# A hybrid attention and S5 block: the scan's output matmuls and the merge transposes held in groups, the rotation phases' low part and two placings on ScalarE, the attention scale in the rotation tables

## The chip, the cores and the metric

One core of a Trainium2 chip. The metric is device time in microseconds (us) of one execution, as the median over repeated runs.

## The reference

One block of a decoder over 256 tokens of width 1024, in float32: an attention branch and a state-space branch run on the same normed input, are merged by gates, and an MLP follows.

```python
h = rms_norm(x, g_mix);  q, k, v, u, g = split(h @ w_in)      # w_in: 1024 x 5632
q, k = rotary(q), rotary(k)                                    # 8 heads of 128
s = q @ k.T * HEAD_DIM ** -0.5                                 # causal, one block of 256
o_a = softmax(s) @ v
# S5: 32 groups of 16 channels, 64 complex states each
x_t = a * x_{t-1} + c * (B u_t);   y = C x + d_skip * u        # a = exp(lam * step), complex
o_b = glu(gelu(y) @ w_glu)
x = x + (sigmoid(g_a) * o_a + sigmoid(g_b) * o_b) @ w_out
x = x + square(relu(rms_norm(x, g_mlp) @ w_up)) @ w_down
out = rms_norm(x, g_final)
```

## The kernel before

**Projections.** Every weight is read once, in units of 128x1024 (512 KB) that `w_load` brings in on SP's queue into five `raw` buffers. `split` (L82 to L85) cuts a unit into two parts: `hi`, a cast on ScalarE (L83), and `lo` = raw - hi, a subtraction on VectorE (L84). Each product is then three matmuls in fp32r (hi·hi, hi·lo, lo·hi): `mm3` (L88 to L90, 256 columns) for q, k, the gate g and up, `tok_mm` (L267 to L269, 512 columns) for v, gb, glu and wo. There are four `hi` and four `lo` buffers. TensorE thus needs, for each unit, a cast of ScalarE and a subtraction of VectorE in time.

**The scan.** The complex recurrence over the 32x64 states is turned into two real scans in a frame that rotates with the state. `prepare` computes the state's constants on VectorE in 128x16 tiles (`s...`), builds the input matrices `Bs` (GpSimd memsets, copies `bpad`, and `place` puts the products `ab` beside it), transposes them on TensorE (`bt`, L471) and copies them to `W2` (L472). A second part builds the output matrices `Wr`, `nWi` and `Dt` with further placings. `tables(m)` makes cos and sin of the phases of a quarter m of the states: angle `ang` in tile `tha` from a high part (`uhi`, four ScalarE activations, L516) and a low part (four VectorE operations, L520), then `cs` and `sn` on ScalarE. `ssm_quad(m)` runs a quarter: matmuls `x` (L539), rotation on VectorE, eight scans (L555, L556), rotation back to `sr` and `si`, and the output matmuls into `y`: `Dt` on the inputs `U2` (L568), `Wr` on `sr` and `nWi` on `si` (L574, 64 columns of the array each).

**Attention.** `rope` turns q and k with the tables `rcos` and `rsin` (L297 to L299), `attn_head` forms scores `s` (L307 to L312), their maximum (L314 to L316), exponentials and the scaled `pr`; `attn_pt` transposes `pr` (`pt`, L330), `attn_out` multiplies with v (`o`).

**Merge.** For each of four groups of channels, glu is projected, gated, multiplied with the gate `thb`, and transposed in four transposes `mt` (L662).

**Order.** The parts are written in the order of `ORDER`, but each engine's final order is set when the kernel is built: a scheduler simulates the engines and issues by priority (weight splits at `SPLIT_PRIO`, attention at `ATT_PRIO`). On the chip every engine then runs its list strictly in that order. A different operation or dependency can therefore move instructions far from the edited lines.

Of the kernel before, what the change touches and what calls it, by code (L numbers as in the profile page):

```python
# [16 lines left out]
P = 128  # L17
# [31 lines left out]
def build(ctx, tc, dr, out):  # L49
# [182 lines left out]
    rs_par = rs.rearrange("p (j e) -> p e j", e=2).unsqueeze(1).to_broadcast([P, 2, 2, P])  # L232
    for c in range(2):
        V.tensor_mul(u[:, 2 * c : 2 * c + 2], by_parity(u_acc[:, c]), rs_par)
    V.tensor_mul(rcos, cos_c, rs)
    V.tensor_mul(rsin, sin_c, rs)
    for q in range(4):
        for e in range(2):
            r = 64 * (q % 2) + 32 * e
# [59 lines left out]
        V.tensor_add(o, o, sw)  # L299
        return o  # L300

    scale = P ** -0.5
    mixA = p1.tile([P, KD, T], F32, name="mixA")

    def attn_head(q, k, j):
        s = att_bank("s").rearrange("p a b -> p (a b)")
        PE.matmul(s[:, 0:128], q[:, j, 0:128], k[:, j, 0:128], start=True, stop=False,  # L307
                  skip_group_check=True)
        PE.matmul(s[:, 0:128], ident_b, tri_b, start=False, stop=True, skip_group_check=True)
        PE.matmul(s[:, 128:384], q[:, j, 128:256], k[:, j, :], start=True, stop=False,  # L310
                  skip_group_check=True)
        PE.matmul(s[:, 256:384], ident_b, tri_b, start=False, stop=True, skip_group_check=True)  # L312
        st = p1.tile([P, 6], F32, tag="st", bufs=2, name="st")
        V.tensor_reduce(st[:, 0:1], s[:, 0:128], axis=mybir.AxisListType.X, op=ALU.max)  # L314
        V.tensor_reduce(st[:, 1:2], s[:, 128:384], axis=mybir.AxisListType.X, op=ALU.max)
        V.tensor_scalar(st[:, 0:2], st[:, 0:2], -scale, None, op0=ALU.mult)  # L316
        pr = p1.tile([P, 384], F32, tag="pr", bufs=2, name="pr")
        act(pr[:, 0:128], s[:, 0:128], AF.Exp, bias=st[:, 0:1], scale=scale,
                     accum_out=st[:, 2:3])
        act(pr[:, 128:384], s[:, 128:384], AF.Exp, bias=st[:, 1:2], scale=scale,  # L320
                     accum_out=st[:, 3:4])
        V.reciprocal(st[:, 4:6], st[:, 2:4])
        S.activation(pr[:, 0:128], pr[:, 0:128], AF.Copy, scale=st[:, 4:5])
        S.activation(pr[:, 128:384], pr[:, 128:384], AF.Copy, scale=st[:, 5:6])
        return pr

    def attn_pt(pr):
        pt = att_bank("pt").rearrange("p a b -> p (a b)")
        for i in range(3):
            PE.transpose(pt[:, i * P : (i + 1) * P], pr[:, i * P : (i + 1) * P], ident)  # L330
        pts = p1.tile([P, 384], F32, tag="pts", bufs=2, name="pts")
        S.copy(pts, pt[:, 0:384])
        return pts

    def attn_out(hp, prs, tha):
        pts = [attn_pt(x) for x in prs]
        o = att_bank("o")
        for j in range(2):
            hd = 2 * hp + j
            PE.matmul(o[:, j, :], v[:, 0, hd * P : (hd + 1) * P], pts[j][:, 0:256],  # L340
                      start=True, stop=False, skip_group_check=True)
# [17 lines left out]
    def prepare():  # L359
# [89 lines left out]
            V.tensor_mul(w, x_r, wide(y_i))  # L449
            (V.tensor_sub if neg_i else V.tensor_add)(o_i, o_i, w)  # L450

        def place(dst, k, src):
            for g in range(2):
                r = slice(64 * g, 64 * (g + 1))
                G.tensor_scalar(dst[r, :, k + 16 * g : k + 16 * (g + 1)], src[r], 1.0, None,
                                    op0=ALU.mult)

        Bs = [p1.tile([P, ST, 64], F32, tag=f"y{c}", name=f"Bs{c}") for c in range(2)]
        ab = [compact(f"ab{c}") for c in range(2)]
# [49 lines left out]
    def rot(name, bufs=1):  # L509
        return p1.tile([P, 4, P], F32, tag=name, bufs=bufs, name=name)  # L510

    def tables(m):
        hi, nlo = ssm[-2:]
        uhi, ang, cs, sn = rot("q", QK), rot("tha", 2), rot("cs", 4), rot("sn", 4)
        for q in range(4):
            S.activation(uhi[:, q, :], tpos, AF.Copy, scale=hi[:, 4 * m + q : 4 * m + q + 1])  # L516
        V.tensor_scalar(ang, uhi, -0.1, MAGIC, op0=ALU.add, op1=ALU.add)
        V.scalar_tensor_tensor(ang, ang, MAGIC, uhi, op0=ALU.subtract, op1=ALU.subtract)
        for q in range(4):
            V.scalar_tensor_tensor(ang[:, q, :], tpos, nlo[:, 4 * m + q : 4 * m + q + 1],  # L520
                                   ang[:, q, :], op0=ALU.mult, op1=ALU.add)
# [8 lines left out]
    def ssm_quad(m):  # L530
# [29 lines left out]
        V.tensor_sub(sr, sr, w)  # L560
        V.tensor_mul(si, b, sn)
        V.tensor_mul(w, d, cs)
        V.tensor_add(si, si, w)
        Wr, nWi, Dt = ssm[1:4]
        y = bank("y", 1, "y")
        for h in range(2):
            p = 2 * m + h
            PE.matmul(y[:, h, 0:P], Dt[:, p, :], U2[:, p, 1 : P + 1], start=(h == 0), stop=False,  # L568
                      skip_group_check=True)
        for i, (w_, s_) in enumerate(((Wr, sr), (nWi, si))):  # L570
            for h in range(2):
                for j in range(2):
                    q = 2 * h + j
                    PE.matmul(y[64 * j : 64 * (j + 1), h, 0:P], w_[:, 4 * m + q, :], s_[:, q, :],  # L574
                              start=False, stop=(i == 1), skip_group_check=True)
        if m < 3:
            S.copy(ysb[:, m], y[:, :, 0:P])
        for q in range(4):
# [66 lines left out]
    for q in range(4):  # L645
        acc = wide_banks(f"glu{q}") if q % 2 else [flat(mm_bank(f"glu{q}{h}")) for h in range(2)]
        for kk_ in range(2):
            wh, wl = w_unit(dr["w_glu"][2 * q + kk_], f"glu{q}{kk_}")
            for k2 in range(2):
                k, w = 2 * kk_ + k2, slice(k2 * 512, (k2 + 1) * 512)  # L650
                for hf in range(2):
                    tok_mm(acc[hf], wh[:, w], wl[:, w], yhl[0][:, 0:4], yhl[0][:, 4:8], k, hf,
                           k == 0, k == 3)
        tp = att_bank(f"mt{q}")
        for hf in range(2):
            sg = p1.tile([P, T], F32, tag=f"ab{hf}", name="sg")
            act(sg, acc[hf][:, 256:512], AF.Tanh, scale=0.5)
            V.scalar_tensor_tensor(sg, sg, 1.0, acc[hf][:, 0:256], op0=ALU.add, op1=ALU.mult)
            tb = thb[q][:, hf, :]
            V.scalar_tensor_tensor(tb, tb, 1.0, sg, op0=ALU.add, op1=ALU.mult)  # L660
            for i in range(2):
                PE.transpose(tp[:, i, hf * P : (hf + 1) * P], tb[:, i * P : (i + 1) * P], ident)  # L662
        two = slice(2 * q, 2 * q + 2)
        V.scalar_tensor_tensor(mixA[:, two, :], tp, 0.5, mixA[:, two, :],
                               op0=ALU.mult, op1=ALU.add)
# [218 lines left out]
```

## Time and profile before

| what | value |
|---|---|
| median of three runs | 397.4 us (397.14 to 397.8) |
| the profiled execution | 396.13 us |
| its span, first to last instruction | 394.3 us |
| mean granted clock of TensorE, share of full | 0.996 |
| TensorE busy | 384.7 us, 98% |
| VectorE busy | 293.0 us, 74% |
| ScalarE busy | 225.9 us, 57% |
| GpSimd busy | 30.9 us, 8% |

The span lies 1.8 us under the profiled execution's time, and that execution 1.3 us under the median. A busy share is an average over the whole span; the kernel's stages differ.

### The profile page before, as it was taken

The page shows a single profiled execution, that of the slowest core. Times are in us where ns is not written, and L with a number is a line of the kernel's source. Part 1 is how long each engine was busy: PE and PEld are TensorE (multiplying, and loading weights), DVE is VectorE, ACT ScalarE, POOL GpSimd, SP SyncE. Part 2 cuts the span into 40 slices and gives each one's busy share as a digit, 9 for nine tenths or more (in the row PEclk, how much of TensorE's full clock was granted, in tenths as well). Part 3 has the DMA queues.
Part 4 walks back from the last instruction along what each step waited for, and adds up shares of the span by engine and source line. Part 5 has one row for each costly group of instructions (what it writes and reads, how often), then busy time and mean ns, then how long its engine had stood idle before and what let it go on. Part 6 is the DMA issues. An engine that isn't in the chain of part 4 may idle for free.

```text
span 394.3 us, 6719 instructions
## 1 busy us (share of the span) xinstructions
PE 384.7 (98%) x2563; PEld 344.5 (87%) x2563; DVE 293.0 (74%) x521; ACT 225.9 (57%) x360; POOL 30.9 (8%) x39
## 2 busy tenths in 40 slices
PE   8999999999999999999999999999999999999993
PEld 5988898999899787888889999999999888888883
DVE  5989999999999996659748677666676444563434
ACT  6857976664366665945636755655655434344313
POOL 4261491000000000000000000000000000000000
PEclk9999999999999999999999999999999999999998
DMA  8994743354625255347396386656556555565202
GB/s 275 374 342 147 248 161 107 108 173 160 215 72 183 91 166 161 118 152 236 140 324 214 106 267 208 193 185 211 187 190 211 173 204 192 184 211 177 89 2 106
DMA packets 23199, 71.57 MB, mean 181 GB/s; under 512 B 2944, under 2 KB 5248, under 8 KB 23168
## 3 DMA queue, kind: packets, MB, share of 16 engines
q1 hardware_dynamic: 20144, 68.92, 52.5%
q10 hardware_dynamic: 3024, 2.23, 2.0%
q8 instruction: 20, 0.33, 0.3%
q14 instruction: 11, 0.09, 0.1%
HBM read 69.18 MB, written 1.05 MB: 178 GB/s over the span
## 4 chain that ended last, share of the span: by engine, by line
PE 79%; DVE 10%; DMA 3%; issue 3%; ACT 2%; POOL 1%; ACTq 1%; SPq 0%
PE up L90 7%; PE up L89 7%; PE up L88 7%; PE dn L734 6%; PE dn L735 6%; PE dn L736 6%; PE gb L269 2%; PE gb L267 2%; PE gb L268 2%; PE glu L269 2%; PE glu L267 2%; PE wo L268 2%; PE glu L268 2%; PE wo L267 2%; PE wo L269 2%
## 5 line engine op out<-in xcount | busy, mean ns | idle before, releaser
L89 PE MATMUL up<-x2l,hi_up 128*128 128x256 f32 x256 | 70.7, 277 | 0.0
L90 PE MATMUL up<-x2h,lo_up 128*128 128x256 f32 x256 | 70.6, 277 | 0.0
L88 PE MATMUL up<-x2h,hi_up 128*128 128x256 f32 x256 | 70.1, 277 | 0.0
L84 DVE TENSOR_TENSOR lo_dn<-raw_dn,hi_dn 128x1024 fp32r<-128x1024 f32 x32 | 39.2, 1225 | 40.4 <-ACT hi_dn L83 40.4
L83 ACT CAST hi_dn<-raw_dn 128x1024 fp32r<-128x1024 f32 x32 | 33.6, 1049 | 49.1 <-PE dn L736 24.6
L84 DVE TENSOR_TENSOR lo_up<-raw_up,hi_up 128x1024 fp32r<-128x1024 f32 x32 | 38.9, 1225 | 23.7 <-ACT hi_up L83 23.7
L83 ACT CAST hi_up<-raw_up 128x1024 fp32r<-128x1024 f32 x32 | 33.3, 1050 | 35.0 <-PE up L89 16.3
L89 PEld LDWEIGHTS up<-x2l,hi_up 128*128 128x128 f32 x256 | 48.1, 188 | 0.0
L90 PEld LDWEIGHTS up<-x2h,lo_up 128*128 128x128 f32 x256 | 48.1, 188 | 0.0
L88 PEld LDWEIGHTS up<-x2h,hi_up 128*128 128x128 f32 x256 | 47.9, 188 | 0.1
L735 PE MATMUL dn<-lo_dn,hh 128*128 128x512 f32 x96 | 37.4, 390 | 0.0
L736 PE MATMUL dn<-hi_dn,hl 128*128 128x512 f32 x96 | 37.4, 390 | 0.0
L734 PE MATMUL dn<-hi_dn,hh 128*128 128x512 f32 x96 | 37.4, 389 | 0.0
L734 PEld LDWEIGHTS dn<-hi_dn,hh 128*128 128x128 f32 x96 | 18.0, 188 | 3.7
L736 PEld LDWEIGHTS dn<-hi_dn,hl 128*128 128x128 f32 x96 | 18.0, 188 | 3.7
L735 PEld LDWEIGHTS dn<-lo_dn,hh 128*128 128x128 f32 x96 | 18.0, 188 | 3.6
L89 PE MATMUL g<-xgl,hi_g 128*128 128x256 f32 x64 | 18.5, 290 | 0.0
L90 PE MATMUL q<-xgh,lo_q 128*128 128x256 f32 x64 | 18.1, 283 | 0.0
L88 PE MATMUL k<-xgh,hi_k 128*128 128x256 f32 x64 | 18.1, 283 | 0.0
L90 PE MATMUL g<-xgh,lo_g 128*128 128x256 f32 x64 | 18.1, 282 | 0.0
L89 PE MATMUL q<-xgl,hi_q 128*128 128x256 f32 x64 | 18.0, 282 | 0.0
L88 PE MATMUL g<-xgh,hi_g 128*128 128x256 f32 x64 | 18.0, 282 | 0.0
(274 smaller groups left out, 1020.4 us busy)
## 6 DMA issues: line engine op xcount, KB each, us to landing
raw_up<-w_up SPq DMA_DIRECT2D x32, 512.0 KB, 3.4
raw_dn<-w_down SPq DMA_DIRECT2D x32, 512.0 KB, 3.3
raw_v<-w_in SPq DMA_DIRECT2D x8, 512.0 KB, 5.9
raw_q<-w_in SPq DMA_DIRECT2D x8, 512.0 KB, 3.3
raw_k<-w_in SPq DMA_DIRECT2D x8, 512.0 KB, 3.5
raw_g<-w_in SPq DMA_DIRECT2D x8, 512.0 KB, 4.0
raw_gb<-w_in SPq DMA_DIRECT2D x8, 512.0 KB, 3.5
raw_glu<-w_glu SPq DMA_DIRECT2D x8, 512.0 KB, 3.3
```

The source lines that it names most:

```text
L83: ins = S.copy(hi, x).ins
L84: V.tensor_sub(lo, x, hi.bitcast(F32))
L88: PE.matmul(o, wh, xh, start=first, stop=False, **kw)
L89: PE.matmul(o, wh, xl, start=False, stop=False, **kw)
L90: PE.matmul(o, wl, xh, start=False, stop=last, **kw)
L267: PE.matmul(acc, xh[:, k, rows], wh, start=first, stop=False)
L268: PE.matmul(acc, xh[:, k, rows], wl, start=False, stop=False)
L269: PE.matmul(acc, xl[:, k, rows], wh, start=False, stop=last)
L734: PE.matmul(acc, xh, wh[:, w], start=(k == lead), stop=False, skip_group_check=True)
L735: PE.matmul(acc, xh, wl[:, w], start=False, stop=False, skip_group_check=True)
L736: PE.matmul(acc, xl, wh[:, w], start=False, stop=(k == end), skip_group_check=True)
```

## The change

1. The output matmuls of quarters 0 to 2 (`Dt`, `Wr`, `nWi`) all depend on the last operation that makes `si`, so that they issue together.
2. The four transposes `mt` of a merge group all depend on the second half's product `merged`.
3. The same kind of hold is written for the transposes and the output of a head pair, with a list cut by `[: hp < 0]`, which is empty for every pair.
4. `tables`: the low part is made by four ScalarE activations into a tile `ulo` and one VectorE addition, in place of four VectorE operations.
5. The placing of `ab` in `Bs` goes from GpSimd to ScalarE copies; the other placings stay.
6. The scale 128^-0.5 is split over `rcos` and `rsin`; the exponentials and the maximum need no scale any more.

```diff
+    def after(ins, others, reason):
+        for o in others:
+            tc.add_manual_dep(ins, o.name, mybir.DependencyInfo(
+                mybir.DependencyClass.Sync, mybir.DependencyReason.DATA), reason=reason)
...
-    V.tensor_mul(rcos, cos_c, rs)
-    V.tensor_mul(rsin, sin_c, rs)
+    V.scalar_tensor_tensor(rcos, cos_c, P ** -0.25, rs, op0=ALU.mult, op1=ALU.mult)
+    V.scalar_tensor_tensor(rsin, sin_c, P ** -0.25, rs, op0=ALU.mult, op1=ALU.mult)
...
-        V.tensor_reduce(st[:, 0:1], s[:, 0:128], axis=mybir.AxisListType.X, op=ALU.max)
-        V.tensor_reduce(st[:, 1:2], s[:, 128:384], axis=mybir.AxisListType.X, op=ALU.max)
-        V.tensor_scalar(st[:, 0:2], st[:, 0:2], -scale, None, op0=ALU.mult)
+        V.tensor_reduce(st[:, 0:1], s[:, 0:128], axis=mybir.AxisListType.X, op=ALU.max,
+                        negate=True)
+        V.tensor_reduce(st[:, 1:2], s[:, 128:384], axis=mybir.AxisListType.X, op=ALU.max,
+                        negate=True)
...
-        pts = [attn_pt(x) for x in prs]
+        pts = [attn_pt(x, [scaled[2 * hp + j]][: hp < 0]) for j, x in enumerate(prs)]
...
-        def place(dst, k, src):
+        def place(dst, k, src, urgent=False):
             for g in range(2):
                 r = slice(64 * g, 64 * (g + 1))
-                G.tensor_scalar(dst[r, :, k + 16 * g : k + 16 * (g + 1)], src[r], 1.0, None,
-                                    op0=ALU.mult)
+                to = dst[r, :, k + 16 * g : k + 16 * (g + 1)]
+                if urgent:
+                    with tc.high_priority(ATT_PRIO):
+                        S.copy(to, src[r])
+                else:
+                    G.tensor_scalar(to, src[r], 1.0, None, op0=ALU.mult)
...
-            place(Bs[c], 32, ab[c])
+            place(Bs[c], 32, ab[c], urgent=True)
...
+        ulo = rot("ulo")
...
             S.activation(uhi[:, q, :], tpos, AF.Copy, scale=hi[:, 4 * m + q : 4 * m + q + 1])
+            S.activation(ulo[:, q, :], tpos, AF.Copy, scale=nlo[:, 4 * m + q : 4 * m + q + 1])
...
-        for q in range(4):
-            V.scalar_tensor_tensor(ang[:, q, :], tpos, nlo[:, 4 * m + q : 4 * m + q + 1],
-                                   ang[:, q, :], op0=ALU.mult, op1=ALU.add)
+        V.tensor_add(ang, ang, ulo)
...
-        V.tensor_add(si, si, w)
+        done = V.tensor_add(si, si, w).ins
...
-            PE.matmul(y[:, h, 0:P], Dt[:, p, :], U2[:, p, 1 : P + 1], start=(h == 0), stop=False,
-                      skip_group_check=True)
+            after(PE.matmul(y[:, h, 0:P], Dt[:, p, :], U2[:, p, 1 : P + 1], start=(h == 0),
+                             stop=False, skip_group_check=True).ins, [done][: m < 3], "y together")
...
-            V.scalar_tensor_tensor(tb, tb, 1.0, sg, op0=ALU.add, op1=ALU.mult)
+            merged = V.scalar_tensor_tensor(tb, tb, 1.0, sg, op0=ALU.add, op1=ALU.mult).ins
+            tbs.append(tb)
+        for hf in range(2):
             for i in range(2):
-                PE.transpose(tp[:, i, hf * P : (hf + 1) * P], tb[:, i * P : (i + 1) * P], ident)
+                after(PE.transpose(tp[:, i, hf * P : (hf + 1) * P],
+                                    tbs[hf][:, i * P : (i + 1) * P], ident).ins,
+                       [merged][: 1], "a group's transposes together")
```

**What moves on VectorE.** The place is between the splits of V's units 5 and 6 (`lo_v_5`, `lo_v_6`); `tha` is an angle, `s...` a constant of the states, `ab` the products for the input matrices. Before, two rows of the first table's low part, the split of unit 5 and, five rows on, that of unit 6:

```order
L520 SCALAR_TENSOR_TENSOR tha_656<-cst_89,s38_538,tha_656 128x128 x2
L384 TENSOR_TENSOR s55_572<-s29_520,s47_556 128x16
L520 SCALAR_TENSOR_TENSOR tha_656<-cst_89,s38_538,tha_656 128x128 x2
L84 TENSOR_TENSOR lo_v_5_407<-raw_v_5_404,hi_v_5_406 128x1024
L480 TENSOR_SCALAR bc_462<-bc_462 128x256
L518 SCALAR_TENSOR_TENSOR tha_777<-tha_777,q_776 128x512
L384 TENSOR_TENSOR s57_576<-s55_572,s47_556 128x16
L389 SCALAR_TENSOR_TENSOR s60_582<-s55_572,s54_570 128x16
L84 TENSOR_TENSOR lo_v_6_425<-raw_v_6_422,hi_v_6_424 128x1024
```

Now, the rows that end with the split of unit 6:

```order
L534 TENSOR_SCALAR tha_857<-q_856 128x512
L456 TENSOR_TENSOR ab0_612<-bc_462,s61_584 128x256
L459 TENSOR_TENSOR ab1_613<-bc_462,s61_584 128x256
L395 TENSOR_TENSOR s68_598<-s66_594,s67_596 128x16
L395 TENSOR_TENSOR s72_606<-s70_602,s71_604 128x16
L535 SCALAR_TENSOR_TENSOR tha_857<-tha_857,q_856 128x512
L458 TENSOR_TENSOR ab0_612<-ab0_612,cw_614 128x256
L536 TENSOR_TENSOR tha_780<-tha_780,ulo_778 128x512
L395 TENSOR_TENSOR s69_600<-s68_598,s62_586 128x16
L395 TENSOR_TENSOR s73_608<-s72_606,s62_586 128x16
L84 TENSOR_TENSOR lo_v_6_425<-raw_v_6_422,hi_v_6_424 128x1024
L239 TENSOR_TENSOR u_287<-u_acc_110,xg0_64 128x512 x2
```

The split of unit 6 has moved behind the whole chain of constants that leads to `ab0`, behind three parts of two tables and the low part's addition; twelve rows ahead of it stand behind it in the list of before.

**What moves on TensorE at `bt`.** `bt` are the transposes of the input matrix `Bs0`, q the first projected pair. Before, they stand near the end of q:

```order
L89 MATMUL q_869<-xgl_106,hi_q_9_902 128x256
L90 MATMUL q_869<-xgh_105,lo_q_9_903 128x256
L88 MATMUL q_869<-xgh_105,hi_q_9_902 128x256
L471 MATMUL bt_631<-cst_89,Bs0_610 128x128 x4
L471 MATMUL bt_637<-cst_89,Bs0_610 128x128 x4
L89 MATMUL q_869<-xgl_106,hi_q_9_902 128x256
L90 MATMUL q_869<-xgh_105,lo_q_9_903 128x256
```

Now they stand after the first two matmuls of V's unit 7:

```order
L272 MATMUL v40_384<-hi_v_7_442,xgh_105 128x512
L272 MATMUL v41_385<-hi_v_7_442,xgh_105 128x512
L486 MATMUL bt_631<-cst_89,Bs0_610 128x128 x4
L486 MATMUL bt_637<-cst_89,Bs0_610 128x128 x4
L88 MATMUL q_875<-xgh_105,hi_q_8_878 128x256
L89 MATMUL q_875<-xgl_106,hi_q_8_878 128x256
L273 MATMUL v40_384<-lo_v_7_443,xgh_105 128x512
L274 MATMUL v40_384<-hi_v_7_442,xgl_106 128x512
L273 MATMUL v41_385<-lo_v_7_443,xgh_105 128x512
```

They have moved forward past the rest of that unit and nearly all of q. The scores of the first pair of heads (`s`, eight matmuls) have moved the other way: before, nothing but 13 matmuls of the gate g stands between the second part of `Dt`'s matmuls and them; now they stand 33 matmuls of g later, between two parts of the matmuls `x` of quarter 1, and the second quarter's scores likewise stand inside an `x`.

**What moves on TensorE at y.** y is the output of quarter 0, `pt` a transpose of attention, `o` the attention's output. Before, its `Wr` matmuls stand in two pieces between transposes in k of the second pair of heads (units 16, 17), and its `nWi` matmuls 40 rows on:

```order
L330 MATMUL pt_1124<-cst_89,pr_1048 128x128
L574 MATMUL y_755<-sr_746,Wr_673 64x128 x2
L330 MATMUL pt_1124<-cst_89,pr_1048 128x128 x2
L574 MATMUL y_755<-sr_746,Wr_673 64x128 x2
L90 MATMUL k_1268<-xgh_105,lo_k_16_1272 128x256
L88 MATMUL k_1268<-xgh_105,hi_k_16_1271 128x256
L89 MATMUL k_1268<-xgl_106,hi_k_16_1271 128x256
...
L90 MATMUL k_1268<-xgh_105,lo_k_17_1302 128x256
L574 MATMUL y_755<-si_747,nWi_674 64x128 x4
L88 MATMUL k_1268<-xgh_105,hi_k_17_1301 128x256
L89 MATMUL k_1268<-xgl_106,hi_k_17_1301 128x256
```

Now its ten matmuls stand in one piece, in q of the third pair of heads:

```order
L88 MATMUL q_1342<-xgh_105,hi_q_21_1375 128x256
L583 MATMUL y_757<-U2_288,Dt_706 128x128 x2
L589 MATMUL y_757<-sr_748,Wr_675 64x128 x4
L589 MATMUL y_757<-si_749,nWi_676 64x128 x4
L89 MATMUL q_1342<-xgl_106,hi_q_21_1375 128x256
L90 MATMUL q_1342<-xgh_105,lo_q_21_1376 128x256
```

From w_out on the order on every engine is the one of before, and so is the order of the DMAs on SP's queue. On ScalarE the copies to `Bs0` stand behind the cast of V's unit 7, those to `Bs1` between DMA issues for `U2`, and the sixteen new activations of `ulo` with the tables; the copies from `bt` to `W20` follow the first two pairs of v's copies.

## Rows read from the trace of the kernel before

**Rows 1.** The page of the profiled execution: busy time of each engine with its share of the span; then, in 40 equal slices of the span and in tenths, the busy share of VectorE and the clock granted to TensorE.

```profile
PE 384.7 (98%) x2563; PEld 344.5 (87%) x2563; DVE 293.0 (74%) x521; ACT 225.9 (57%) x360; POOL 30.9 (8%) x39
...
DVE  5989999999999996659748677666676444563434
...
PEclk9999999999999999999999999999999999999998
```

**Rows 2.** The waits of TensorE over the whole span, by what was waited for: engine, the waiting tile and line, the releaser; total us, times, longest.

```profile
PE s L307 <- DVE k L299: 0.7, 1, 0.7
PE bt L471 <- POOL Bs L455: 0.7, 1, 0.7
PE pt L330 <- ACT pr L323: 0.5, 1, 0.5
```

**Rows 3.** The timeline of TensorE at those three waits: start, duration of one, engine, line, operation, tiles and shapes, how many; in brackets the idle time ahead and its releaser. Matmuls overlap, so a step is read from one start to the next.

```profile
46.84 0.28 PE L88 MATMUL q<-xgh,hi_q 128*128 128x256 f32 x1
47.83 1.09 PE L471 MATMUL bt<-cst,Bs 128*128 128x128 f32 x8 [0.71 <-POOL Bs L455]
...
64.08 0.28 PE L90 MATMUL g<-xgh,lo_g 128*128 128x256 f32 x1
65.10 0.46 PE L307 MATMUL s<-k,q 128*128 128x128 f32 x2 [0.74 <-DVE k L299]
...
77.88 0.28 PE L89 MATMUL q<-xgl,hi_q 128*128 128x256 f32 x1
78.65 0.33 PE L330 MATMUL pt<-cst,pr 128*128 128x128 f32 x1 [0.49 <-ACT pr L323]
```

**Rows 4.** The timeline of VectorE from 28.9 to 36.7 us, around the splits `lo_v` of units 5 and 6. Each operation starts shortly before the one ahead of it has fully ended, so here too a step is read from start to start.

```profile
28.94 0.41 DVE L517 TENSOR_SCALAR tha<-q 128x512 f32<-128x512 f32 x1
29.27 0.60 DVE L520 SCALAR_TENSOR_TENSOR tha<-cst,s,tha 128x128 f32<-128x128 f32 x2
...
29.89 0.96 DVE L520 SCALAR_TENSOR_TENSOR tha<-cst,s,tha 128x128 f32<-128x128 f32 x2
30.77 1.21 DVE L84 TENSOR_TENSOR lo_v<-raw_v,hi_v 128x1024 fp32r<-128x1024 f32 x1
31.91 0.28 DVE L480 TENSOR_SCALAR bc<-bc 128x256 f32<-128x256 f32 x1
32.11 0.68 DVE L518 SCALAR_TENSOR_TENSOR tha<-tha,q 128x512 f32<-128x512 f32 x1
32.72 0.16 DVE L384 TENSOR_TENSOR s<-s,s 128x16 f32<-128x16 f32 x1
...
32.89 1.21 DVE L84 TENSOR_TENSOR lo_v<-raw_v,hi_v 128x1024 fp32r<-128x1024 f32 x1
34.02 0.60 DVE L520 SCALAR_TENSOR_TENSOR tha<-cst,s,tha 128x128 f32<-128x128 f32 x2
...
34.80 1.27 DVE L234 TENSOR_TENSOR u<-u_acc,xg 128x512 f32<-128x512 f32 x2
36.00 0.40 DVE L235 TENSOR_TENSOR rcos<-cst,xg 128x256 f32<-128x256 f32 x1
36.34 0.41 DVE L236 TENSOR_TENSOR rsin<-cst,xg 128x256 f32<-128x256 f32 x1
```

**Rows 5.** The timeline of TensorE at V's unit 6: its first matmul and its third.

```profile
35.91 0.39 PE L267 MATMUL v<-hi_v,xgh 128*128 128x512 f32 x1
...
36.36 0.40 PE L269 MATMUL v<-hi_v,xgl 128*128 128x512 f32 x1
```

**Rows 6.** The timeline of GpSimd: the copying in of `bpad`, and the four placings of the input matrices.

```profile
27.83 3.49 POOL L463 TENSOR_SCALAR Bs<-bpad 128x512 f32<-128x512 f32 x2 [0.52 <-DMA bpad<-bpad]
44.51 5.60 POOL L455 TENSOR_SCALAR Bs<-ab 64x256 f32<-64x256 f32 x4 [13.19 <-DVE s L384]
```

**Rows 7.** The timeline of ScalarE: four small activations of a table's high part, three of the eight DMA issues for `U2`, and its idle time before the swap of k.

```profile
28.53 1.28 ACT L516 ACTIVATE q<-cst,s 128x128 f32<-128x128 f32 x4 [1.98 <-DVE tha L518]
...
39.05 1.92 ACTq L241 DMA_DIRECT2D U<-u  x3
...
59.93 0.58 ACT L294 COPY sw<-k 64x512 f32<-64x512 f32 x1 [2.78 <-PE dps L495]
```

**Rows 8.** The timeline of TensorE at three places where matmuls of the scan or of attention stand in the stream of projections: the first `Dt` matmuls of the output y of quarter 0, the second transposes of head 1 with the `Wr` matmuls of that y, and its `nWi` matmuls.

```profile
62.27 0.37 PE L89 MATMUL g<-xgl,hi_g 128*128 128x256 f32 x1
62.48 0.38 PE L568 MATMUL y<-U,Dt 128*128 128x128 f32 x2
...
81.47 0.27 PE L330 MATMUL pt<-cst,pr 128*128 128x128 f32 x1
81.68 0.44 PE L574 MATMUL y<-sr,Wr 128*64 128x128 f32 x4
82.05 0.44 PE L330 MATMUL pt<-cst,pr 128*128 128x128 f32 x2
...
88.32 0.28 PE L90 MATMUL k<-xgh,lo_k 128*128 128x256 f32 x1
88.53 0.66 PE L574 MATMUL y<-si,nWi 128*64 128x128 f32 x8
89.11 0.38 PE L88 MATMUL k<-xgh,hi_k 128*128 128x256 f32 x1
89.34 0.28 PE L89 MATMUL k<-xgl,hi_k 128*128 128x256 f32 x1
```

More of the change, by code (lines that the diff above doesn't have):

```diff
@@ L300, in rope @@
         return o
-    scale = P ** -0.5
     mixA = p1.tile([P, KD, T], F32, name="mixA")
+    scaled = []
     def attn_head(q, k, j):
@@ L313, in attn_head @@
         st = p1.tile([P, 6], F32, tag="st", bufs=2, name="st")
-        V.tensor_reduce(st[:, 0:1], s[:, 0:128], axis=mybir.AxisListType.X, op=ALU.max)
-        V.tensor_reduce(st[:, 1:2], s[:, 128:384], axis=mybir.AxisListType.X, op=ALU.max)
-        V.tensor_scalar(st[:, 0:2], st[:, 0:2], -scale, None, op0=ALU.mult)
+        V.tensor_reduce(st[:, 0:1], s[:, 0:128], axis=mybir.AxisListType.X, op=ALU.max,
+                        negate=True)
+        V.tensor_reduce(st[:, 1:2], s[:, 128:384], axis=mybir.AxisListType.X, op=ALU.max,
+                        negate=True)
         pr = p1.tile([P, 384], F32, tag="pr", bufs=2, name="pr")
-        act(pr[:, 0:128], s[:, 0:128], AF.Exp, bias=st[:, 0:1], scale=scale,
+        act(pr[:, 0:128], s[:, 0:128], AF.Exp, bias=st[:, 0:1],
                      accum_out=st[:, 2:3])
-        act(pr[:, 128:384], s[:, 128:384], AF.Exp, bias=st[:, 1:2], scale=scale,
+        act(pr[:, 128:384], s[:, 128:384], AF.Exp, bias=st[:, 1:2],
                      accum_out=st[:, 3:4])
@@ L323, in attn_head, with attn_pt @@
         S.activation(pr[:, 0:128], pr[:, 0:128], AF.Copy, scale=st[:, 4:5])
-        S.activation(pr[:, 128:384], pr[:, 128:384], AF.Copy, scale=st[:, 5:6])
+        scaled.append(S.activation(pr[:, 128:384], pr[:, 128:384], AF.Copy, scale=st[:, 5:6]).ins)
         return pr
-    def attn_pt(pr):
+    def attn_pt(pr, last):
         pt = att_bank("pt").rearrange("p a b -> p (a b)")
         for i in range(3):
-            PE.transpose(pt[:, i * P : (i + 1) * P], pr[:, i * P : (i + 1) * P], ident)
+            after(PE.transpose(pt[:, i * P : (i + 1) * P], pr[:, i * P : (i + 1) * P], ident).ins,
+                   last, "a head's transposes together")
         pts = p1.tile([P, 384], F32, tag="pts", bufs=2, name="pts")
-        S.copy(pts, pt[:, 0:384])
+        copied.append(S.copy(pts, pt[:, 0:384]).ins)
         return pts
+    copied = []
     def attn_out(hp, prs, tha):
-        pts = [attn_pt(x) for x in prs]
+        pts = [attn_pt(x, [scaled[2 * hp + j]][: hp < 0]) for j, x in enumerate(prs)]
         o = att_bank("o")
@@ L339, in attn_out @@
             hd = 2 * hp + j
-            PE.matmul(o[:, j, :], v[:, 0, hd * P : (hd + 1) * P], pts[j][:, 0:256],
-                      start=True, stop=False, skip_group_check=True)
+            after(PE.matmul(o[:, j, :], v[:, 0, hd * P : (hd + 1) * P], pts[j][:, 0:256],
+                             start=True, stop=False, skip_group_check=True).ins,
+                   copied[-1:][: hp < 0], "a pair's outputs together")
             PE.matmul(o[:, j, 128:256], v[:, 1, hd * P : (hd + 1) * P], pts[j][:, 256:384],
@@ L573, in ssm_quad @@
                     q = 2 * h + j
-                    PE.matmul(y[64 * j : 64 * (j + 1), h, 0:P], w_[:, 4 * m + q, :], s_[:, q, :],
-                              start=False, stop=(i == 1), skip_group_check=True)
+                    after(PE.matmul(y[64 * j : 64 * (j + 1), h, 0:P], w_[:, 4 * m + q, :],
+                                     s_[:, q, :], start=False, stop=(i == 1),
+                                     skip_group_check=True).ins, [done][: m < 3], "y together")
         if m < 3:
@@ L654, in build @@
         tp = att_bank(f"mt{q}")
+        tbs = []
         for hf in range(2):
```

## The prediction

> **What bounds the kernel now.** I read the page first. TensorE is busy 98% of the span and its clock is granted at 9 tenths or more, 2.4 GHz, until the last slice [rows 1]; only what removes TensorE's work or its waits can shorten the kernel. So the next view is its waits: after the start there are three, each once [rows 2]. The timeline gives their real price, since the idle time it prints is short of what is lost. In the stream of 256-column matmuls one starts about every 0.117 us, so the step from the last matmul to the waiting one, less 0.115, is lost. At `bt`: 47.83 - 46.84 - 0.115 = 0.88 us, for GpSimd's placing; at `s`: 65.10 - 64.08 - 0.115 = 0.90, for VectorE's rope of k; at `pt`: 78.65 - 77.88 - 0.115 = 0.66, for ScalarE's scaled `pr` [rows 3]. Together 2.44 us. All else that VectorE, ScalarE and GpSimd do lies under the matmuls, and counts only where it comes late for one.
>
> **What the change removes.**
>
> *The wait at `bt`: -0.88.* The four placings take 5.60 us on GpSimd from 44.51 on [rows 6], begun when VectorE has `ab0`. Now `ab0` is made ahead of `lo_v_6` and the copies are ScalarE's. I have no row of a 64x256 copy there; its bounds are 0.3 us a copy (the smaller 128x128 activation, 1.28 us for four [rows 7]) and 0.58 (the 64x512 copy of the swap [rows 7]). Two take 0.6 to 1.2; `Bs0` is done by 37 to 38. TensorE reaches the moved `bt` after two matmuls of unit 7, at about 40. Two microseconds of cover, and the wait is gone. The second input matrix's transposes stand at about 49, and `Bs1` is ready near 45.
>
> *The wait at `s`: -0.90.* The scores stand 33 gate matmuls later, 33 x 0.1145 = 3.8 us; some `x` goes ahead of them and two pieces of `Dt` (0.5) leave, so TensorE gets there near 67.9. On VectorE four operations of 0.60 now stand ahead of k's last addition, and the low part's two pairs of 0.60, which overlap to some 1.05 [rows 4], become 0.60: that is ready at 65.0 + 2.4 - 0.45 = 67.0. Margin 0.9 us.
>
> *The wait at `pt`: -0.66.* It moves 28 matmuls back (to about 80.2), while the scaled `pr` comes near 79.7. Margin 0.5 us, the thinnest with that of the held y of quarter 0 (TensorE at 90.2, `si` at 89.6). The holds of the other quarters have 0.8 us or more by the same reckoning.
>
> *The pieces of y and `mt`: -0.95.* Matmuls that use 64 columns of the array cost something on entering and on leaving: 88.53 - 88.32 = 0.21 and 89.34 - 89.11 = 0.23, each some 0.1 over the pace, for eight in 0.58 in between [rows 8]. Between two transposes the same is paid again: the four `Wr` matmuls take 0.37 where half of 0.58 is 0.29 [rows 8]. A second group soon after a first costs 0.09 too, 62.48 - 62.27 against 0.117 [rows 8]. Quarter 0 has three such groups and two pieces of `Dt` before and one piece after: four switches and one 0.09, about 0.5 us. Quarters 1 and 2 go from three groups (one inside an `x`) to one: 0.4 and 0.35. Against that the scores now stand inside `x` for quarters 1 and 2, two switches more each, 0.4 together. `mt` saves one or two times 0.09: 0.1. Net 0.95. Bounds: 0.4 if half of the switches cost nothing in the new places, 1.3 if those around the scores cost nothing.
>
> **What the change adds.**
>
> *A new wait for `lo_v_6`: +1.0.* On VectorE, from 28.94: the table's addition 0.60 (as one of the two at 34.80 to 36.00), `bc` 0.20, an angle step 0.33, three constants 0.25, a second angle step 0.61, `lo_v_5` 1.14, and 0.35 because GpSimd copies until 31.32 [rows 6] and VectorE's low-part pairs beside it last 0.96 instead of 0.60 [rows 4]. That is 32.5. Then come four products of 128x256 at 0.34, ten constants at 0.085, two angle steps (0.33 and 0.61) and an addition of 0.60: 3.7 us, 36.15; `lo_v_6` takes 1.13 and ends at 37.3 [rows 4]. Before it ended at 34.02. TensorE wants it at the third matmul of unit 6, 36.36 [rows 5]. Late by 0.94, with the signal 1.0. Without GpSimd's 0.35 it is 0.6; with as much again, 1.35. Behind it on VectorE wait u, `rcos`, `rsin` and `lo_v_7`, which ends at 40.7; the eight `bt` transposes and two q matmuls now ahead of unit 7's first low part cover it, to 41.3. So this wait happens once.
>
> *ScalarE's own load.* Sixteen activations at 0.3 are 4.8 us, four copies 1.2 to 2.3. ScalarE is busy 57% [rows 1] and still had 2.78 us idle at 59.9 [rows 7]; the load is hidden unless it delays a cast or a copy. The tightest is `W20`'s copy, whose PSUM bank the second `bt` needs: it stands behind eight DMA issues of 0.64 [rows 7]. An issue runs beside the operation ahead of it (three of them, 39.05 to 40.97, beside a cast from 39.03 on), so I count what outlasts it. The copy ends near 48.6, TensorE asks at 48.9. Cost nothing, margin 0.25.
>
> *The scale.* `rcos` and `rsin` become scalar-tensor-tensor operations of the same shape, which the angle step shows at the price of the plain one (0.61 against 0.60); eight tiny operations go. Nothing on the path.
>
> The Trainium skill, "Perfetto Trace Analysis", section "Optimizing Scalar/DVE Operations", speaks against the sixteen small activations: fixed overhead per instruction, so larger ones are better on a saturated engine. Four pieces of 1.28 us replace four on VectorE of like length, and ScalarE isn't saturated on average; by that rule the danger is ScalarE in this stretch, which is the slower rival below. "SBUF — State Buffer", section "Who interferes with whom", says that VectorE with two inputs and GpSimd exclude each other at a shared port pair; the 0.96 against 0.60 [rows 4] agrees. By it taking 5.6 us of placings off GpSimd speeds VectorE up by about a microsecond near 45 to 50, where TensorE doesn't wait for VectorE.
>
> *Sum.* -2.44 - 0.95 + 1.0, and +0.3 for margins of a few tenths that I can't all have right: -2.1 us. From the profiled execution's 396.13 that is 394.0; against the median of 397.4, 395.3. A measurement of this kernel tells changes of 0.2%, 0.8 us, from none.
>
> **The rivals.**
>
> *Same.* The thin margins fail: VectorE or ScalarE is a microsecond later than reckoned in 60 to 90, so that `s`, `pt` or y wait as before. Each of them gives back up to its 0.5 to 0.9; two of them with a longer `lo_v_6` (1.35) give 1.8 back: 397.1. For it: VectorE is busy 9 tenths and more in every slice from 30 to 148 us [rows 1], so what is late there is hardly made up, and 0.5 us is little. Against: it loses 0.45 us per table and gets rid of GpSimd's neighbour for 5.6 us. 0.20.
>
> *Slower: ScalarE becomes the bound between 37 and 62.* If DMA issues don't run beside the work ahead of them, the `W20` copy comes 2 us later and the second `bt` waits 1.75; from there the casts `hi_g_12` and `hi_g_13` are late too, since both stand behind `W20`, four table activations and `ulo` of the fourth table. At 2 us late the gain is used up; from 3 us it is slower by more than 0.8: 398.3. For it: ScalarE executes in order, and every 0.3 us piece stands ahead of something. Against: the idle time of 2.78 us, which all must be used first [rows 7]. 0.14.
>
> *It does not do what it says.* The holds on `pt` and on the attention's output have empty lists, so these stay in pieces: that part saves nothing, and none is counted. If the y hold too saved only 0.4, the time is 395.9, still faster; within the likeliest case.
>
> **How the numbers follow.** The likeliest, 0.66: 395.3, its own range 394.2 to 396.5 (savings 0.4 to 1.3, new wait 0.6 to 1.35, margins 0 to 0.9). Same 0.20, slower 0.14. The range for 8 in 10 reaches into the same case and to the edge of the slower: 393.9 to 398.0.
>
> **What would show it.** Right: in TensorE's waits `s`, `bt` and `pt` are gone and one of about a microsecond for `lo_v` stands near 36.4; y has one row of `Dt`, `Wr` and `nWi` for quarters 0 to 2. Wrong: a wait on `hi_g` or `bt` with ScalarE as releaser between 48 and 58 (slower), or on `s`, `pt` or y with VectorE or ScalarE (same); or a `lo_v` wait of 2 us or more.

## The result and the profile after

The changed kernel takes 393.62 us where the kernel before takes 396.99 (medians of 13 runs each, taken in turns); the ratio is 0.9925, 95% interval 0.9905 to 0.9945. That is 3.0 us less by the ratio, 2.1 were forecast; by it the median of 397.4, from which the prediction counted, becomes 394.4, inside its range of 393.9 to 398.0. The profiled execution has a span of 392.2 us against 394.3. The page's first line and TensorE's waits of the changed kernel (engine, waiting tile and line, releaser; total us, times, longest):

```profile
PE 382.8 (98%) x2563; PEld 343.7 (88%) x2563; DVE 288.7 (74%) x501; ACT 231.8 (59%) x380; POOL 29.6 (8%) x35
```

```profile
PE u_acc L186 <- DVE lo_u L84: 1.5, 2, 0.9
...
PE up L89 <- DVE x2l L718: 0.2, 1, 0.2
```

The three waits of [rows 2] are gone; TensorE has nothing to wait for between the opening (`u_acc` and, in the rows left out, `hot`) and the MLP (`up`). TensorE's timeline at the three places shows why:

```profile
40.72 0.62 PE L272 MATMUL v<-hi_v,xgh 128*128 128x512 f32 x2
41.18 1.03 PE L486 MATMUL bt<-cst,Bs 128*128 128x128 f32 x8
...
68.30 0.28 PE L90 MATMUL g<-xgh,lo_g 128*128 128x256 f32 x1
68.51 0.71 PE L554 MATMUL x<-U,W 64*128 64x128 f32 x6
69.15 0.49 PE L313 MATMUL s<-k,q 128*128 128x128 f32 x2
...
81.19 0.28 PE L88 MATMUL k<-xgh,hi_k 128*128 128x256 f32 x1
81.31 0.27 PE L337 MATMUL pt<-cst,pr 128*128 128x128 f32 x1
```

`bt` follows unit 7 of V by the pace (41.18 - 40.72 is two matmuls of 512 columns); the scores start inside `x` 0.64 us behind its start; `pt` follows its neighbour by 0.12. In [rows 3] the same steps were 0.99, 1.02 and 0.77.

The opening of this execution ran late: V's unit 6 began at 37.88, not 35.91 [rows 5]. The lag is there at the first matmul of V's unit 0 already, 20.85 against 18.88, and that stands ahead of everything that differs: VectorE's list is the same up to 28.9 us and TensorE's up to `bt`, while ScalarE's first `ulo` runs at 26.3. Over the profiled executions of all kernels here unit 6 began between 35.5 and 37.9. So this is scatter of the opening. To leave it out, I count from the first matmul of unit 6 to the end of the span: before 394.3 - 35.91 = 358.4, after 392.2 - 37.88 = 354.3. That is 4.1 us less.

### The profile page after: what moved, and what is told of

It is laid out like the page before. It is cut to its first block, busy times and chain, and to the rows that moved or that the text cites. A ratio compares the mean times of both kernels' runs of the same rounds, so it can differ in the third digit from the quotient of the medians.

```text
span 392.2 us, 6719 instructions
## 1 busy us (share of the span) xinstructions
PE 382.8 (98%) x2563; PEld 343.7 (88%) x2563; DVE 288.7 (74%) x501; ACT 231.8 (59%) x380; POOL 29.6 (8%) x35
## 4 chain that ended last, share of the span: by engine, by line
PE 92%; DMA 3%; DVE 3%; issue 1%; ACT 0%; SPq 0%; DVEq 0%
PE up L89 7%; PE up L88 7%; PE up L90 7%; PE dn L757 6%; PE dn L756 6%; PE dn L755 6%; PE u_acc L186 3%; DMA x2t<-x 2%; PE gb L272 2%; PE g L88 2%; PE k L88 2%; PE q L88 2%; PE g L89 2%; PE q L89 2%; PE v L272 2%; PE g L90 2%
## 5 line engine op out<-in xcount | busy, mean ns | idle before, releaser
L89 PE MATMUL k<-xgl,hi_k 128*128 128x256 f32 x64 | 18.1, 283 | 0.0
L88 PE MATMUL q<-xgh,hi_q 128*128 128x256 f32 x64 | 17.9, 280 | 0.0
L90 PE MATMUL k<-xgh,lo_k 128*128 128x256 f32 x64 | 17.9, 279 | 0.0
```

The lines of the kernel that those rows point to most:

```text
L88: PE.matmul(o, wh, xh, start=first, stop=False, **kw)
L89: PE.matmul(o, wh, xl, start=False, stop=False, **kw)
L90: PE.matmul(o, wl, xh, start=False, stop=last, **kw)
```

## The experiments

Each ratio below is to the kernel before, run in turns with it on the same chip.

**The changed kernel again.** No edit.

> The changed kernel once more. In its first profile the opening stage of TensorE (u_acc) ran 2 us late, so that the wait for lo_v_6 nearly vanished behind it. Theory (the late lo_v_6 is paid when the opening is on time): with the first matmul of V's unit 6 near 35.9 the step to the third part of that unit shows a wait of 0.7 to 1.1 us; from that first matmul to the end of the span it is then about 355, against 358.4 before and 354.3 in the first profile. Rival (lo_v_6 moves with the opening and is never waited for): no such wait however early the opening, and 354.3 again.

Ratio 0.9908 (0.9872 to 0.9944), span 391.0. VectorE's timeline, then TensorE's, at unit 6:

```profile
36.16 1.21 DVE L84 TENSOR_TENSOR lo_v<-raw_v,hi_v 128x1024 fp32r<-128x1024 f32 x1
37.29 1.28 DVE L239 TENSOR_TENSOR u<-u_acc,xg 128x512 f32<-128x512 f32 x2
```

```profile
36.88 0.62 PE L272 MATMUL v<-hi_v,xgh 128*128 128x512 f32 x2
37.42 0.50 PE L273 MATMUL v<-lo_v,xgh 128*128 128x512 f32 x1
```

`lo_v_6` ran from 36.16 to 37.29: the prediction had 36.15 and 37.3. TensorE came at 36.88 + 0.46 = 37.34, so only 0.08 us were lost beyond the pace. From 36.88 to the end are 354.1 us, as in the first profile. Neither expectation was met to the letter, since the opening was late again; the next run, with the same list on VectorE up to there, has an early one.

**Low part alone on ScalarE.**

```diff
+            S.activation(ulo[:, q, :], tpos, AF.Copy, scale=nlo[:, 4 * m + q : 4 * m + q + 1])
...
+        V.tensor_add(ang, ang, ulo)
```

> The kernel before with the low part of the phases on ScalarE alone; the placing stays on GpSimd. Theory of the order: lo_v_6 is late as in the changed kernel (0.7 to 1.1 us of wait unless the opening is late), bt follows unit 7 of V in two pieces and waits little, scores stand 48 and pt 97 matmuls later and don't wait; y in pieces: 1.3 to 1.8 us less. Rival: ScalarE's added 4.8 us come back as waits on ScalarE's copies or casts between 37 and 62, 0 to 2 us more than before; or only the scores' wait goes, 0.9 less.

Ratio 1.0262 (1.0226 to 1.0299): 10 us slower. TensorE's timeline at unit 6, and its waits:

```profile
35.47 0.62 PE L267 MATMUL v<-hi_v,xgh 128*128 128x512 f32 x2
37.35 0.50 PE L268 MATMUL v<-lo_v,xgh 128*128 128x512 f32 x1 [1.26 <-DVE lo_v L84]
```

```profile
PE pt L330 <- ACT pr L323: 7.6, 2, 4.8
PE v L268 <- DVE lo_v L84: 1.3, 1, 1.3
```

Here the opening was early, 35.47, and the wait for `lo_v_6` is there: 37.35 - 35.47 less two steps of 0.23 is 1.42 us. So the price depends on how two times meet, when TensorE comes and when `lo_v_6` ends. But the 10 us come from something that no expectation held: 7.6 us of waiting at `pt`, the transposes of the last heads.

**Placing alone on ScalarE.**

```diff
+                    with tc.high_priority(ATT_PRIO):
+                        S.copy(to, src[r])
```

> The kernel before with the placing of the two input matrices on ScalarE alone. Theory of the order: bt, scores and pt all stand about 21, 21 and 51 matmuls later on TensorE, VectorE's list is the old one up to lo_v_7; so all three waits go, no wait for lo_v_6 comes, y stays in pieces: 2.4 us less, most of the whole change from one edit. Rival (each wait belongs to one edit): only the wait at bt goes, 0.9 us less.

Ratio 1.0153 (1.0117 to 1.0190): 6 us slower. The three early waits are indeed all gone, from one edit. In their place stands one at the end of the gate gb's projection. TensorE's timeline there, one row of VectorE's, ScalarE's, and windows with busy time by engine and TensorE's granted clock (the last column but two):

```profile
161.50 0.50 PE L330 MATMUL pt<-cst,pr 128*128 128x128 f32 x3
168.92 0.47 PE L330 MATMUL pt<-cst,pr 128*128 128x128 f32 x1 [6.92 <-ACT pr L323]
...
171.33 0.63 PE L268 MATMUL glu<-lo_glu,yhl 128*128 128x512 f32 x1
171.75 0.63 PE L267 MATMUL glu<-hi_glu,yhl 128*128 128x512 f32 x1
...
174.12 0.40 PE L268 MATMUL glu<-lo_glu,yhl 128*128 128x512 f32 x1
174.35 0.39 PE L267 MATMUL glu<-hi_glu,yhl 128*128 128x512 f32 x1
```

```profile
164.51 0.17 DVE L322 RECIPROCAL st<-st 128x2 f32<-128x2 f32 x1 [0.98 <-ACT pr L107]
```

```profile
163.93 0.46 ACT L107 ACTIVATE pr<-s,st 128x256 f32<-128x256 f32 x1
...
164.50 1.28 ACT L101 ACT_TABLE_LOAD   x1
165.79 1.33 ACT L107 ACTIVATE yT<-yT 128x256 f32<-128x256 f32 x4
167.03 1.54 ACT L107 ACTIVATE thb<-gb,rs_half 128x256 f32<-128x256 f32 x4
168.46 0.41 ACT L323 ACTIVATE pr<-pr,st 128x128 f32<-128x128 f32 x1
```

```profile
170.00:175.00 5.00, 5.00 (x18) 4.16 (x17) 1.16 (x4) 1.18 (x3) 0.00 (x0) 0.66 0.00 0
175.00:180.00 5.00, 5.00 (x24) 4.17 (x23) 2.24 (x3) 1.67 (x3) 0.00 (x0) 1.00 0.00 0
```

The last head's scores reach TensorE at 160.68, behind all 768 projection matmuls of v, q, k, g and gb that come ahead of glu. Nothing is left to run while the maximum, the exponential (163.93), the load of the next function table, eight activations for y and the gates, and at last the scaling of `pr` (168.46) go through ScalarE in that order. Before, the last scores were at 152.98 with 44 matmuls of gb behind them. The wait of 7.1 us costs more than itself: the granted clock falls to 0.66 of full in the next 5 us, and a matmul of 512 columns starts every 0.43 us where it was 0.23, until 173.9. A fall to 0.66 over 5 us is worth some 1.7 us (an estimate, a third of 5); 7.1 + 1.7 less the 2.4 of the three early waits is 6.4, and from the start of unit 6 to the end this execution takes 364.8 us against 358.4.

About half of the wait is ScalarE's own order. The scaling of `pr` needs the reciprocal `st`, done at 164.7, but the table load and the eight activations stand ahead of it and take until 168.46. So it is in every kernel here that waits at the end of gb: the scaling starts 3.1 to 4.6 us behind the end of its reciprocal, with the table load and such activations in between. The kernel before (3.4 us) and the changed one (2.6 us) have the load and some of the rest there too, but matmuls of gb hide it. No run puts the scaling ahead of them.

**Holds alone.**

```diff
+            after(PE.matmul(y[:, h, 0:P], ... ).ins, [done][: m < 3], "y together")
...
+                after(PE.transpose(tp[:, i, hf * P : (hf + 1) * P], ... ).ins, [merged][: 1], ... )
```

> The kernel before with the holds on y and on mt alone. Theory (a wait goes when the order puts the waiting matmul later, whatever edit moved it): the wait at bt stays at 0.9, the scores move only 4 matmuls and keep 0.4 of their 0.9, pt moves 9 matmuls and keeps none; with 1 to 1.5 us for the pieces, 1.5 to 2.5 us in all. Rival (each wait belongs to one edit, the holds only join pieces): all three waits stay, 1 to 1.5 us less.

Ratio 1.0203 (1.0166 to 1.0240): 8 us slower. TensorE's waits:

```profile
PE pt L335 <- ACT pr L328: 6.7, 3, 5.1
...
PE s L312 <- ACT cs L527: 0.9, 1, 0.9
PE bt L476 <- POOL Bs L460: 0.6, 1, 0.6
```

The early waits stayed, as the rival said, though both expected a gain; all of the 6.7 us at `pt` but about 0.5 are at the end of gb again, with no matmul of gb behind the last scores.

**The change without the holds.** `[done][: m < 3]` and `[merged][: 1]` become empty lists.

> The changed kernel without the holds on y and mt; low part and placing stay on ScalarE. Theory of cover (a wait of about 7 us at the last transposes pt comes when fewer than some 31 matmuls of the gate gb, 0.2285 us each, stand behind the last scores on TensorE; the parts alone had none behind them, the kernel before has 44, the changed one 39): 40 stand there, so no such wait, and the three early waits are gone as in the changed kernel. What is lost is the joining of the pieces: 1.0 to 1.6 us more than the changed kernel, 2 less than before. Rival (the holds are needed for a good end): a wait of 3 to 7 us at pt, and slower than before.

Ratio 0.9960 (0.9945 to 0.9975): 1.6 us less than before, as expected. No wait at the end and none at `bt`, `s` or `pt`. At unit 6 TensorE, with the opening at 36.57, waits again, and VectorE's row shows that the end of `lo_v_6` moves too, here to 37.83:

```profile
36.57 0.62 PE L272 MATMUL v<-hi_v,xgh 128*128 128x512 f32 x2
37.89 0.50 PE L273 MATMUL v<-lo_v,xgh 128*128 128x512 f32 x1 [0.70 <-DVE lo_v L84]
```

```profile
36.62 1.21 DVE L84 TENSOR_TENSOR lo_v<-raw_v,hi_v 128x1024 fp32r<-128x1024 f32 x1
```

That step loses 0.86 us. From 36.57 to 392.5 are 355.9; less 0.86, 355.1, against 354.0 for the changed kernel's second execution without its 0.08 and 354.3 for its first. So the holds are worth 0.8 to 1.0 us in place.

**The change with the placing back on GpSimd.**

> The changed kernel with the placing of the input matrices back on GpSimd. Theory of cover: 14 matmuls of gb stand behind the last scores, 3.2 us where about 8 are needed from the scores to the scaled probabilities less 0.9 for the scores themselves: a wait of 3 to 5 us at the last pt, the early waits small, so 1 to 3 us slower than before. Rival (the placing is worth its own wait at bt and no more): 0.9 us more than the changed kernel, 2 less than before.

Ratio 1.0175 (1.0159 to 1.0191). TensorE's largest waits:

```profile
PE pt L337 <- ACT pr L330: 3.3, 1, 3.3
PE gb L272 <- DVE tha L360: 1.5, 1, 1.5
```

With 14 matmuls behind the last scores the wait at `pt` is 3.3 us (3.5 in the step), as expected; another 1.5 us stand at gb. The time is 6.9 us over before where 1 to 3 were expected. A part of that is the clock: it is granted at 0.50 from 168.6 to 170 and at 0.59 from 170 to 175. That costs some 2.8 us (an estimate from these two shares); the rest is not accounted for.

**The placing alone, with the last pair of heads raised.**

```diff
+            with tc.high_priority(600 if n == 3 else 0):
                 qk[n] = (rope(proj_pair(8 + 6 * n, "q"), "q"), rope(proj_pair(10 + 6 * n, "k"), "k"))
...
-            with tc.high_priority(ATT_PRIO):
+            with tc.high_priority(ATT_PRIO if n < 3 else 900):
                 prs[n] = [attn_head(q, k, j) for j in range(2)]
```

> The kernel before with the placing on ScalarE alone, as in the earlier run, and besides the projections, ropes and scores of the last pair of heads raised in priority, so that 34 matmuls of gb stand behind the last scores instead of none. Theory of cover: 7.8 us of matmuls hide the last pair's softmax, the wait of 7.1 us at pt shrinks to under 1, the early waits stay away: 1 to 2.5 us faster than before. Rival (ScalarE's or VectorE's load at the end of the scan makes the wait, not the order): 4 us or more at pt again, slower than before.

Ratio 1.0145 (1.0129 to 1.0162). The wait at the end of gb is gone, as the theory of cover said, but the time is not: TensorE's waits now begin with

```profile
PE o L340 <- ACT pts L332: 2.4, 1, 2.4
PE y L578 <- DVE si L567: 1.8, 1, 1.8
```

and nearly all lie between 76 and 126 us. The first pair's transposes, `y` and outputs now stand together from 99 to 108 us with no projection matmul between them, where the placing alone has 18 between that pair's `pt` and `o`. So cover is short again, at another place: enough of it at the end of gb does not make an order good.

**Low part of tables 0 and 1 back on VectorE.**

> The changed kernel with the low part of tables 0 and 1 back on VectorE, of 2 and 3 on ScalarE. VectorE's list then has lo_v_6 ten rows earlier; bt stands 24 matmuls later, the rest nearly as in the changed kernel with 40 matmuls of cover. Theory (lo_v_6 is a floor for TensorE at about 37.3 us, paid only when the opening is earlier than 36.9): no floor any more; the same as the changed kernel when the opening is late, up to 1 us less when it is on time: median 0 to 0.8 us less. Rival (the low part on ScalarE is needed in the first tables): a wait of 0.5 or more comes back at bt, s or pt, 0.3 to 2 us more than the changed kernel.

Ratio 0.9919 (0.9899 to 0.9940), median 392.99. No wait at all behind the opening, V's unit 6 at 36.05, where `lo_v_6` had ended at 35.59; from there to the end 354.2 us, as in the changed kernel. Its interval and those of the changed kernel's two measurements overlap: no difference shown, though its profiled span, 390.3, is the shortest.

**The change without the scale edit.** The maximum, its scaling by `-scale`, the exponentials, `rcos` and `rsin` as before; the empty lists of the third item go too, and with them no dependency.

> The changed kernel with the scale left in the maximum and the exponentials as before (the rotation tables carry none); all other edits stay. Theory (the scale edit takes one small VectorE operation, and with it one passage through VectorE's full list, out of every head's chain of scores, maximum, exponentials, transposes and output; without it the scheduler puts the last scores at the end of gb): both scores of the last pair stand behind all 768 matmuls, so waits of 8 to 12 us about pt, and 4 to 8 us slower than before. Rival (as predicted, the scale edit is worth nothing): within 0.3 us of the changed kernel.

Ratio 1.0236 (1.0176 to 1.0296). TensorE's first wait:

```profile
PE pt L335 <- ACT pr L328: 8.0, 2, 7.8
```

No matmul of gb stands behind the last scores, as expected; the loss, 9.4 us, is more than the 4 to 8 expected.

**The scale edit alone.**

> The kernel before with the scale edit alone. The waits at bt (same place) and scores (same place) stay, 0.8 to 0.9 each; pt stands 18 matmuls earlier, 2.1 us, against a chain shorter by an operation: a wait of 1 to 2.5 there; the last scores have 61 matmuls of gb behind them and no wait at the end. Theory: within 1.5 us of before on either side. Rival (one operation less per head is worth its own time): 0.2 us less.

Ratio 1.0007 (0.9978 to 1.0036). Three early waits, no late one:

```profile
PE bt L472 <- POOL Bs L456: 0.9, 1, 0.9
...
PE s L307 <- DVE k L299: 0.7, 1, 0.7
PE pt L331 <- ACT pr L324: 0.6, 1, 0.6
```

**Scale edit and placing.**

> The kernel before with the scale edit and the placing on ScalarE, without the low part and the holds. Last scores with 66 matmuls of gb behind them, so no wait at the end; bt 21 and the first scores 21 matmuls later, no waits there; pt where it was before, but TensorE comes 1.8 us earlier: a wait of 0.5 to 2 there and perhaps at y. Theory of cover: 0.5 to 2 us faster than before, where the placing alone was 6 slower. Rival (the placing on ScalarE is bad in itself): 4 us slower or more.

Ratio 1.0247 (1.0199 to 1.0294); the theory of cover was right on the end of gb (no wait there) and wrong on the time. TensorE's waits:

```profile
PE pt L331 <- ACT pr L324: 4.3, 1, 4.3
PE up L89 <- DVE x2l L702: 2.4, 1, 2.4
PE xt L697 <- DVE x2t L695: 1.3, 1, 1.3
```

The transposes `pt` of the second pair now wait 4.3 us, until 116.6, after which the granted clock is 0.50 for 5 us. Their head's exponentials are done at 110.9, but its reciprocal runs on VectorE at 115.9, behind a weight split and operations of the scan: a chain that has to pass VectorE's full list. The waits at `xt` and `up` come from the MLP's input `x2t`, whose DMA is issued at 209.1 (199.1 before). Here the scheduler has put it behind two more loads of `raw_up` on SP's queue; in its old place, 0.7 us behind the load at 202.5, it would have come some 6 us earlier (an estimate).

**The matmuls x together.**

```diff
+        with tc.high_priority(2 * ATT_PRIO):
             for h in range(2): ...  PE.matmul(x[:, j, i, h, :], ... )
```

and the low part of table 0 on VectorE.

> The changed kernel with the matmuls x of each quarter raised in priority, so that no scores split them, and the low part of table 0 back on VectorE. lo_v_6 stands ten rows earlier on VectorE (no floor at 37.3 us), last scores with 44 matmuls behind them, fewer pieces: two splits of x at 0.47 each go. Theory: 0.5 to 1.5 us less than the changed kernel, 0.987 to 0.990 of before. Rival (y of quarter 0 now stands 15 matmuls earlier, 1.7 us, and waits for si): the same as the changed kernel or up to 1 us more.

Ratio 1.0153 (1.0107 to 1.0199). No wait at the end of gb nor at y of quarter 0, but these:

```profile
PE up L89 <- DVE x2l L725: 3.1, 1, 3.1
PE o L350 <- ACT pts L340: 2.2, 1, 2.2
```

VectorE stands idle 4.6 us for `x2t`, whose DMA is issued at 204.0 (196.4 in the changed kernel), one load of `raw_up` later on SP's queue than before, and `x2l` comes late by it. The idle time alone does not show that: it is 3.65 us in the changed kernel run again, where TensorE loses nothing. But these last two kernels are the only ones here with this DMA moved on the queue, and the only ones with waits of over 1 us at `up`. No version tried is shown to beat the changed kernel.

## Why the prediction was right

**The three waits, -2.44: right.** All three are gone by the mechanism given: the waiting matmuls stand later on TensorE or what they wait for is earlier. The prediction read the places from the order of the whole change and counted at `s` on the low part's saving too; the placing alone, with the low part left on VectorE, removes all three, because its order moves the scores and `pt` as well.

**The wait for `lo_v_6`, +1.0: right place, price too high.** VectorE's path was right: from the table's addition to the start of `lo_v_6` it takes 7.2 to 7.5 us in the six profiled executions that have this list, where the prediction has 7.21 (28.94 to 36.15). One reading in it is weak: the 0.96 us of a low-part pair is put down to GpSimd's copies, but the pair ahead of it, beside the same copies, lasts 0.60 [rows 4]. The step that failed took both ends from one execution: TensorE's 36.36 and VectorE's 28.94. Both scatter, each by itself, and the loss is what is left between them:

| run | unit 6 begins on TensorE | `lo_v_6` ends | lost |
|---|---|---|---|
| low part alone | 35.47 | 37.30 | 1.42 |
| placing back on GpSimd | 36.50 | 37.42 | 0.51 |
| without the holds | 36.57 | 37.83 | 0.86 |
| without the scale edit | 36.87 | 37.58 | 0.30 |
| the changed kernel again | 36.88 | 37.37 | 0.08 |
| the changed kernel | 37.88 | 38.26 | 0 |

The mean is 0.53 us. A fixed floor at 37.3, as two of the expectations have it, is not what the six show.

**The pieces, -0.95: too small.** For each stretch of float32 matmuls in the stream behind 25 us I took the step from the projection matmul ahead to the second one behind, less the pace. Summed, that is 40.70 us before, 2.43 of it the waits, and 36.73 after: 1.5 us saved. The y of quarter 0 in the changed kernel, on TensorE's timeline:

```profile
91.22 0.28 PE L88 MATMUL q<-xgh,hi_q 128*128 128x256 f32 x1
91.34 0.60 PE L583 MATMUL y<-U,Dt 128*128 128x128 f32 x4
91.87 0.66 PE L589 MATMUL y<-sr,Wr 128*64 128x128 f32 x8
92.36 0.61 PE L589 MATMUL y<-si,nWi 128*64 128x128 f32 x8
92.90 0.39 PE L89 MATMUL q<-xgl,hi_q 128*128 128x256 f32 x1
93.12 0.28 PE L90 MATMUL q<-xgh,lo_q 128*128 128x256 f32 x1
```

From 91.22 to 93.12 less two matmuls at 0.117 is 1.67 us. Its parts before were 0.55, 1.09 and 0.79, 2.43 in sum (one of them in [rows 8]); so 0.76 is saved where I put 0.5. Half of the difference is a rate: eight matmuls on 64 columns take 0.58 us [rows 8], 0.0725 each, while these sixteen in one run take 91.87 to 92.90, 0.064 each, and I counted switches alone. Quarter 3, which has no hold, gains 0.55 too, since its `Wr` matmuls no longer stand in two pieces. Against that the scores inside `x` cost 0.47 a time, not 0.2: that stretch takes 3.59 us, where the scores alone took 1.83 and an `x` alone 1.29.

**Margins, +0.3: not needed.** `s`, `pt` and y never waited. With -2.44, -1.5 and 0 to +0.08 the sum is -3.9; the two traces give 4.1 and 4.3 from unit 6 on. The medians differ by 3.4, the ratio makes it 3.0. Executions in which TensorE comes to `lo_v_6` earlier than in these two give part of it back; how often that was so in the runs without a profile is not on record. All three sizes were off to the same side, so the gain came out larger than forecast; none made up for another.

**The scale edit, "nothing on the path": wrong, though it did not enter the sum.** Without it the same change is 2.4% slower than before. It drops an operation between each head's maximum and exponential, which had to pass VectorE's list. In the kernel before, head 4's maximum is taken at 128.2 and the small operation behind it runs at 130.8, while ScalarE's exponential waits for it:

```profile
128.18 0.41 DVE L315 TENSOR_REDUCE st<-s 128x1 f32<-128x256 f32 x1
...
130.84 0.16 DVE L316 TENSOR_SCALAR st<-st 128x2 f32<-128x2 f32 x1
```

```profile
131.04 0.37 ACT L107 ACTIVATE pr<-s,st 128x128 f32<-128x128 f32 x1 [1.18 <-DVE st L316]
```

Alone the edit is worth nothing that the runs show (1.0007); what it does in the changed kernel goes through the order, which without it has no matmul of gb behind the last scores. In the runs here a kernel was slow by the end of gb whenever 14 or fewer matmuls of gb stood behind the last scores, and never with 34 or more.

**The rivals.** ScalarE did not become the bound between 37 and 62; no wait has it as releaser there. The real danger was in none of the rivals: of the eleven kernels here that differ from the changed one, eight are 1.4% to 2.6% slower than before, five of them by waits at the end of gb, from 160 us on, three by waits elsewhere. That the change as a whole escapes the first could be read in the order (39 matmuls of gb behind the last scores, 44 before), but the prediction did not read it there. In this it was lucky: it was right on the terms that it counted, and nothing in it showed that this larger one would be nothing.

Left open: whether a shorter chain of a head's own operations, above all with the scaling of `pr` ahead of the table load on ScalarE, would make every order safe. The runs that have the late waits differ in order from those that have none, and no run changes that chain alone at the end of gb.

## What to carry to other kernels

Where a scheduler sets the order, the parts of a change don't add up: here three of the four were 6 to 10 us slower alone than none, the fourth the same, and all together 3 us faster. Read the order to the end of every stage: count what stands behind the last operation that starts a serial chain (here a softmax), since that is what hides it, and look at what stands inside the chain on each engine. And a wait near the opening, between two engines that each start when their data come, has no one price: take it over the scatter of both, not at one instant.

## What the runs showed of the hardware

A wait of TensorE can cost more than its length, by the clock behind it. Behind 7.1 us (placing alone) the granted clock was 0.66 over the next 5 us, and a 512-column matmul took a step of 0.43 us instead of 0.23. Behind 4.3 us (scale edit and placing) it was 0.50 over 5 us, the lower of the two levels, 1.2 GHz; behind 2.2 us at 120.2 (the matmuls x together) 0.59 over 120 to 122. Behind 1.8 us at 124.7 (the last pair raised), and behind the 0.66 to 0.90 of the kernel before [rows 1], it stayed at full, 2.4 GHz.

Sixteen matmuls on 64 columns in one run take 1.03 us, eight take 0.58 [rows 8], and each run costs some 0.1 on entering and on leaving.
